# Rows set apart in the first loads and in one late store of an elementwise Huber loss, and a full second tile

## The chip, the cores and the metric

The kernel runs on one core of one Trainium2 chip. The metric is the device time of one execution in microseconds (us), lower is better. Below, a "row" is one partition's contiguous run of a tile in DRAM; the core's 16 DMA engines move rows between DRAM and the on-chip memory (SBUF).

## The reference

Two inputs of 8192 x 8192 float32 go in, one array of the same shape comes out, element by element:

```python
def reference(pred, target):
    delta = 1.0
    diff = pred - target
    abs_diff = np.abs(diff)
    return np.where(abs_diff <= delta, 0.5 * diff**2, delta * (abs_diff - 0.5 * delta))
```

So 536.87 MB are read and 268.44 MB are written, and there is no reuse of data.

## The kernel before

The kernel treats each array as one flat run of 67,108,864 floats and cuts it into 37 tiles of 128 rows. Tile `i` takes `128 * widths[i]` consecutive floats; its row `p` is `widths[i]` floats long and goes to partition `p`. The widths are 9408 (`GAP`), then 12000, then 34 times 14592 (`W`), then 6752.

All tiles share one SBUF buffer `mem` of 3 x 14592 + 9408 = 53184 floats per partition. The target of a tile is loaded into its "b" place (`at_b`: the first 14592 floats for even tiles, the next 14592 for odd tiles). The pred goes into its "a" place (`at_a`: even tiles from float 29184 on, odd tiles at the end of the buffer). The difference, and later the result, stand in the b place; the a place also serves as scratch once pred has been subtracted. The a places of neighbouring tiles overlap by up to `R` = 5184 floats; `covered(i)` gives the part of tile `i`'s a place that tile `i + 1` will overwrite. That part is subtracted first (`pieces`, `work`), so that the next tile's pred may be loaded while the rest of tile `i` is still being computed.

The arithmetic of a piece has five instructions on two engines: `subtract` (VectorE tensor_tensor, L95, then ScalarE Abs, L96), `square` (VectorE clamp to [-1, 1], L100, then ScalarE Square with scale sqrt(0.5), L103) and `combine` (VectorE scalar_tensor_tensor, max of |d| - 0.5 and that square, L107).

All loads (L80) and stores (L85) are issued by SyncE (SP), in program order: `load(0)`, `load(1)`, then for each tile `i`: `store(i - 1)`, `load(i + 1)` (inside `work(i)`, after the covered part has been subtracted), and at the end the store of the last tile. A load of pred is issued when the overlapped parts of the a place have been used; a load of target waits until the store that reads the same b place has landed, two tiles back. SP handles its queue in order, so whatever waits holds back everything issued later.

`parts(i)` says in which column ranges a tile is loaded: whole, except for the first tile and the last two (in halves) and the third from the end (two unequal parts). The last tile is also stored in halves. The order of work is written out by hand; waits between engines and DMAs are put in from the regions that overlap. The completion marks of the DMAs issued by SP are kept on eight semaphores in rotation: the ninth DMA uses the semaphore of the first again, and waits until that one has landed.

Of the kernel before, what the change touches and what calls it, by code (L numbers as in the profile page):

```python
# [1 line left out]

# [4 lines left out]


@with_exitstack
def kernel(  # L10
    ctx: ExitStack,
    tc: tile.TileContext,
    pred: bass.AP,
    target: bass.AP,
    out: bass.AP,
):
    nc = tc.nc
    P = 128
    fp32 = mybir.dt.float32
    Alu = mybir.AluOpType  # L20
    Act = mybir.ActivationFunctionType
    SQRT_HALF = 0.70710678118654752

    total = pred.shape[0] * pred.shape[1] // P
    W = 14592
    GAP = 9408
    R = W - GAP
    widths = [GAP, W - R // 2] + [W] * 34
    widths.append(total - sum(widths))
    n = len(widths)  # L30
    starts = [sum(widths[:i]) * P for i in range(n)]

    def block(x, i):
        flat = x.rearrange("r m -> (r m)")
        return flat[starts[i] : starts[i] + P * widths[i]].rearrange("(p m) -> p m", p=P)

    pool = ctx.enter_context(tc.tile_pool(name="memory", bufs=1))
    mem = pool.tile([P, 3 * W + GAP], fp32, name="mem")

    def at_a(i):
        return 3 * W + GAP - widths[i] if i % 2 else 2 * W

    def at_b(i):
        return W if i % 2 else 0

    def covered(i):  # L50

        if i + 1 >= n:
            return (0, 0)
        lo = max(at_a(i), at_a(i + 1))
        hi = min(at_a(i) + widths[i], at_a(i + 1) + widths[i + 1])
        return (lo - at_a(i), hi - at_a(i)) if hi > lo else (0, 0)


    def parts(i):
        w = widths[i]  # L60
        if i == n - 3:
            return [(w - 2 * R, w), (0, w - 2 * R)]
        if i in (0, n - 2, n - 1):
            return halves(w)
        return [(0, w)]

    def halves(w):
        h = w // 32 * 16
        return [(0, h), (h, w)]

    def view(base, lo, hi):
        return mem[:, base + lo : base + hi]

    def load(i):
        order = [(x, part) for part in parts(i) for x in "pt"]
        if i == n - 1:
            order = [(x, part) for x in "pt" for part in parts(i)]
        for x, (lo, hi) in order:
            src, base = (pred, at_a(i)) if x == "p" else (target, at_b(i))
            nc.sync.dma_start(out=view(base, lo, hi), in_=block(src, i)[:, lo:hi])  # L80

    def store(i):
        w = widths[i]
        for lo, hi in halves(w) if i == n - 1 else [(0, w)]:
            nc.sync.dma_start(out=block(out, i)[:, lo:hi], in_=view(at_b(i), lo, hi))  # L85

    def split(lo, hi, size):
        k = -((lo - hi) // size)
        edges = [lo + (hi - lo) * j // k // 16 * 16 for j in range(k)] + [hi]
        return list(zip(edges[:-1], edges[1:]))  # L90


    def subtract(i, lo, hi, at):
        a, d = view(at_a(i), lo, hi), view(at_b(i), lo, hi)
        nc.vector.tensor_tensor(out=d, in0=a, in1=d, op=Alu.subtract)  # L95
        nc.scalar.activation(out=d, in_=d, func=Act.Abs)  # L96

    def square(i, lo, hi, at):
        d, t = view(at_b(i), lo, hi), view(at_a(i) + at, 0, hi - lo)
        nc.vector.tensor_scalar(  # L100
            out=t, in0=d, scalar1=-1.0, scalar2=1.0, op0=Alu.max, op1=Alu.min
        )
        nc.scalar.activation(out=t, in_=t, func=Act.Square, scale=SQRT_HALF)  # L103

    def combine(i, lo, hi, at):
        d, t = view(at_b(i), lo, hi), view(at_a(i) + at, 0, hi - lo)
        nc.vector.scalar_tensor_tensor(  # L107
            out=d, in0=d, scalar=-0.5, in1=t, op0=Alu.add, op1=Alu.max
        )

    def pieces(i, lo, hi):


        c0, c1 = covered(i)
        c0, c1 = max(lo, c0), min(hi, c1)
        if c1 <= c0:
            k = -((lo - hi) // (R // 2 if i < n - 1 else R // 4))
            return [], [(i, x, y, x) for x, y in split(lo, hi, -((lo - hi) // k))]
        x, y = (lo, c0) if c0 > lo else (c1, hi)
        m = max(c1 - c0, (y - x) // 32 * 16)  # L120
        rest = [(x, x + m), (x + m, y)] if y > x + m else [(x, y)]
        return [(i, c0, c1, x)], [(i, x, y, x) for x, y in rest]

    def work(i, then):

        todo, held = [], []
        for part in parts(i):
            first, rest = pieces(i, *part)
            todo += first + rest
            held += first  # L130
        mid, end = [], []
        if held:
            subtract(*todo.pop(0))
        then()
        while todo or mid or end or held:
            if todo:
                piece = todo.pop(0)
                subtract(*piece)
                mid.append(piece)
                if len(mid) < 2 and todo:  # L140
                    continue
            if mid:
                piece = mid.pop(0)
                square(*piece)
                end.append(piece)
                if len(end) < 2 and (todo or mid):
                    continue
            combine(*end.pop(0))
            mid += held
            held = []  # L150

    ctx.enter_context(tc.manual_schedule())

    load(0)
    load(1)
    for i in range(n):
        if i > 0:
            store(i - 1)
        work(i, lambda: load(i + 1) if 0 < i < n - 1 else None)
    store(n - 1)  # L160


# [1 line left out]
_INS = ['pred', 'target']  # L164
_OUTS = [((8192, 8192), 'float32')]


# [23 lines left out]
```

## Time and profile before

| What | Value |
|---|---|
| median of 3 runs | 1867.21 us (1866.58 to 1867.41) |
| the profiled execution | 1866.7 us |
| its span, first to last instruction | 1864.9 us |
| VectorE (DVE) busy | 1408.3 us, 76% |
| ScalarE (ACT) busy | 912.5 us, 49% |
| GpSimd (POOL) busy | 0.2 us |
| DMA under way on the 16 engines | 99.9% of 16 engines' span |
| moved | 805.37 MB, mean 432 GB/s |

The profile comes from one execution, and the program's own instructions fill the span; 1.8 us of the execution's time lie around it. The share of DMA time is a mean over 16 engines: a stretch in which half of them have nothing left counts as half. The packet records behind these sums give start, length and size of each row's transfer, and one 4-byte packet for each engine's completion mark of each DMA.

### The profile page before, as it was taken

To read this page: it belongs to the slowest core of one execution; us is meant where nothing else is said; L and a number is where in the kernel's file an instruction comes from. 1 tells how busy PE (TensorE), PEld (TensorE's weight loads), DVE (VectorE), ACT (ScalarE), POOL (GpSimd) and SP (SyncE) were. 2 spreads that over 40 slices of the span, in tenths; PEclk is the share of its full clock that TensorE was granted. 3 is DMA by queue.
4 is the path that set the end of the run, shared out by engine and by line. 5 is a ranking of instruction groups with operands and counts; after the bars stand their busy time and mean duration, and the time that the engine had idled before them with its cause. 6 is when DMAs were issued, how large, how long until landed. Compare 5 with 4: busy or idle time off the path is not lost.

```text
span 1864.9 us, 960 instructions
## 1 busy us (share of the span) xinstructions
DVE 1408.3 (76%) x357; ACT 912.5 (49%) x239; POOL 0.2 (0%) x4
## 2 busy tenths in 40 slices
DVE  5677777777788777777778877777777887777986
ACT  3455444444555545444455554544445555454554
POOL 0000000000000000000000000000000000000000
DMA  9999999999999999999999999999999999999999
GB/s 421 418 436 431 436 431 432 437 427 436 438 428 434 439 428 435 438 429 433 438 428 436 438 428 435 438 428 436 438 427 437 436 429 437 435 429 436 428 437 393
DMA packets 17287, 805.37 MB, mean 432 GB/s; under 512 B 1920, under 2 KB 1920, under 8 KB 1920
## 3 DMA queue, kind: packets, MB, share of 16 engines
q1 hardware_dynamic: 17280, 805.31, 99.9%
q14 instruction: 7, 0.06, 0.0%
HBM read 536.87 MB, written 268.44 MB: 432 GB/s over the span
## 4 chain that ended last, share of the span: by engine, by line
DMA 56%; DVE 26%; ACT 13%; issue 4%; another core or an unknown queue 1%; SPq 0%; DVEq 0%
DMA mem<-in_target_dram 32%; DMA out_dram<-mem 24%; DVE mem L107 11%; DVE mem L95 11%; ACT mem L103 8%; ACT mem L96 4%; DVE mem L100 3%; SPq L80 0%; DVEq L95 0%
## 5 line engine op out<-in xcount | busy, mean ns | idle before, releaser
L96 ACT ACTIVATE mem<-mem 128x5184 f32<-128x5184 f32 (+8 forms) x119 | 459.2, 3874 | 756.3 <-DVE mem L95 756.2
L95 DVE TENSOR_TENSOR mem<-mem 128x5184 f32<-128x5184 f32 (+8 forms) x119 | 558.5, 4743 | 336.2 <-DMA mem<-in_target_dram 336.2
L107 DVE SCALAR_TENSOR_TENSOR mem<-mem 128x5184 f32<-128x5184 f32 (+8 forms) x119 | 564.4, 4745 | 74.5 <-ACT mem L103 70.6
L103 ACT ACTIVATE mem<-mem 128x5184 f32<-128x5184 f32 (+8 forms) x119 | 456.7, 3864 | 169.2 <-DVE mem L100 169.2
L100 DVE TENSOR_SCALAR mem<-mem 128x5184 f32<-128x5184 f32 (+8 forms) x119 | 292.0, 2453 | 34.9 <-ACT mem L96 29.9
L96 ACT ACT_TABLE_LOAD x1 | 1.3, 1283 | 14.6 <-DMA mem<-in_target_dram 14.6
L175 POOL MEMSET const-bfloat16-1.0<- 128x1 bf16 x1 | 0.1, 103 | 0.0
L175 POOL MEMSET const-uint8-127<- 128x1 uint8 x1 | 0.1, 102 | 0.0
L175 POOL MEMSET const-float32-0.0<- 128x1 f32 x1 | 0.1, 100 | 0.2 <-issue 0.2
L175 POOL MEMSET const-float32-1.0<- 128x1 f32 x1 | 0.1, 99 | 0.0
## 6 DMA issues: line engine op xcount, KB each, us to landing
out_dram<-mem SPq DMA_DIRECT2D x34, 7296.0 KB, 26.5
mem<-in_pred_dram SPq DMA_DIRECT2D x32, 7296.0 KB, 28.7
mem<-in_target_dram SPq DMA_DIRECT2D x32, 7296.0 KB, 34.4
mem<-in_pred_dram SPq DMA_DIRECT2D x2, 3648.0 KB, 27.6
mem<-in_target_dram SPq DMA_DIRECT2D x2, 3648.0 KB, 25.5
mem<-in_pred_dram SPq DMA_DIRECT2D x1, 6000.0 KB, 36.8
mem<-in_target_dram SPq DMA_DIRECT2D x1, 6000.0 KB, 51.5
out_dram<-mem SPq DMA_DIRECT2D x1, 6000.0 KB, 24.6
```

Source lines behind the costliest of these rows:

```text
L95: nc.vector.tensor_tensor(out=d, in0=a, in1=d, op=Alu.subtract)
L96: nc.scalar.activation(out=d, in_=d, func=Act.Abs)
L100: nc.vector.tensor_scalar(out=t, in0=d, scalar1=-1.0, scalar2=1.0, op0=Alu.max, op1=Alu.min)
L103: nc.scalar.activation(out=t, in_=t, func=Act.Square, scale=SQRT_HALF)
L107: nc.vector.scalar_tensor_tensor(out=d, in0=d, scalar=-0.5, in1=t, op0=Alu.add, op1=Alu.max)
L175: nc = _bacc.Bacc("TRN2", target_bir_lowering=False, num_devices=1)
```

## The change

Four places change.

The widths become 9408, 34 times 14592, 13056 and 5696. So the second tile is a full one, the last but one is 13056 instead of 14592 wide, and the last one is 5696 instead of 6752 wide. There are still 37 tiles.

The second tile is loaded in two column parts, 10368 and 4224 wide.

Of the first tile's four loads (pred and target of two halves), the first three are each issued as three DMAs: rows 0 to 111, rows 112 to 119, and rows 120 to 127.

The store of the last tile but one is split by rows. SP stores rows 0 to 111. GpSimd stores rows 112 to 119 and rows 120 to 127, each as two DMAs: the first 16 floats of each row, then the rest of the row.

```diff
-    widths = [GAP, W - R // 2] + [W] * 34
+    widths = [GAP] + [W] * 34 + [13056]
     widths.append(total - sum(widths))
...
     def parts(i):
         w = widths[i]
+        if i == 1:
+            return [(0, 2 * R), (2 * R, w)]
         if i == n - 3:
             return [(w - 2 * R, w), (0, w - 2 * R)]
...
-        for x, (lo, hi) in order:
+        for k, (x, (lo, hi)) in enumerate(order):
             src, base = (pred, at_a(i)) if x == "p" else (target, at_b(i))
-            nc.sync.dma_start(out=view(base, lo, hi), in_=block(src, i)[:, lo:hi])
+
+            apart = i == 0 and k < 3
+            for r0, r1 in [(0, 112), (112, 120), (120, 128)] if apart else [(0, P)]:
+                nc.sync.dma_start(
+                    out=mem[r0:r1, base + lo : base + hi], in_=block(src, i)[r0:r1, lo:hi]
+                )
 
     def store(i):
         w = widths[i]
+        if i == n - 2:
+
+            todo = [(nc.sync, 0, 112, 0, w)]
+            for r in (112, 120):
+                todo += [(nc.gpsimd, r, r + 8, 0, 16), (nc.gpsimd, r, r + 8, 16, w)]
+            for queue, r0, r1, lo, hi in todo:
+                queue.dma_start(
+                    out=block(out, i)[r0:r1, lo:hi],
+                    in_=mem[r0:r1, at_b(i) + lo : at_b(i) + hi],
+                )
+            return
         for lo, hi in halves(w) if i == n - 1 else [(0, w)]:
             nc.sync.dma_start(out=block(out, i)[:, lo:hi], in_=view(at_b(i), lo, hi))
```

## The prediction

> **What bounds the kernel now.** I read the page first: its sums, then the chain of waits.
>
> ```profile
> span 1864.9 us, 960 instructions
> ...
> DVE 1408.3 (76%) x357; ACT 912.5 (49%) x239; POOL 0.2 (0%) x4
> ...
> DMA packets 17287, 805.37 MB, mean 432 GB/s; under 512 B 1920, under 2 KB 1920, under 8 KB 1920
> ...
> q1 hardware_dynamic: 17280, 805.31, 99.9%
> ...
> DMA 56%; DVE 26%; ACT 13%; issue 4%; another core or an unknown queue 1%; SPq 0%; DVEq 0%
> ```
>
> The engines have slack, the DMA engines none: 99.9% of their time is taken. The chain runs through DVE and ACT for 39%, but only because one releaser at a time is followed back; behind each such piece the DMA queue is still full. So a change pays or costs only where DMA engines stand still, slow down, or end unevenly. Next, the table by stretches (busy DVE, ACT, POOL, clock, DMA share, GB/s), for where that happens:
>
> ```profile
> 0.00:1.60 1.60, 0.00 (x0) 0.00 (x0) 0.20 (x4) 1.00 0.00 0
> 1.60:15.00 13.40, 0.36 (x1) 0.39 (x1) 0.00 (x0) 1.00 1.01 414
> ...
> 51.00:55.00 4.00, 0.00 (x0) 0.00 (x0) 0.00 (x0) 1.00 1.07 343
> ...
> 410.00:1500.00 1090.00, 827.10 (x190) 530.57 (x126) 0.00 (x0) 1.00 1.00 434
> ...
> 1859.00:1861.00 2.00, 0.00 (x0) 0.00 (x0) 0.00 (x0) 1.00 0.85 358
> 1861.00:1863.60 2.60, 0.00 (x0) 0.00 (x0) 0.00 (x0) 1.00 0.36 151
> 1863.60:1864.90 1.30, 0.00 (x0) 0.00 (x0) 0.00 (x0) 1.00 0.00 0
> ```
>
> Nothing moves for 1.6 us, the rate is low in the first stretch and around 51 to 55 us (343 GB/s), steady at 434 later, and in the last 4.6 us the share falls to 0.85 and 0.36: engines have run out one by one. The packet records give the rest. A row's time is bytes / 27.2 per ns + about 9 ns: 0.70 us for 18,816 bytes, 1.39 for 37,632, 2.154 for 58,368, 0.505 for 13,504. Each DMA has 16 completion marks, 8 rows for each. The 16 marks of one DMA lie 0.84 us apart at 25 us, 0.92 at 54, 1.85 at 150, 2.84 at 254, 3.3 at 409, and the last ones 3.47 (1860.14 to 1863.62, mean 1861.82). So the engines, which have equal work, drift apart by slow packets, nearly all before 410 us and where loads turn into stores (51, 147, 200, 251 us), and the last engine ends 1.8 us after the mean. Slow packets sum to 2.9 us per engine, 1.1 of it in the one stall at 51 to 55 us.
>
> Last, how early each transfer is queued (timeline of SP's issues, then the chain near the end):
>
> ```profile
> 106.69 0.33 SPq L80 DMA_DIRECT2D mem<-in_pred_dram  x1
> 115.30 0.33 SPq L80 DMA_DIRECT2D mem<-in_target_dram  x1
> 143.40 0.34 SPq L85 DMA_DIRECT2D out_dram<-mem  x1
> ```
>
> ```profile
> 1789.19 33.52 DMA out_dram<-mem
> 1822.72 12.08 DMA mem<-in_target_dram
> ```
>
> The pred load issued at 106.69 has the store before it ending at 113.65 on the first engine: 7.0 us of cover. The store issued at 143.40 finds the load before it ending from 148.29 on: 4.9 us. The first load shows about 1.0 us from issue (0.73) to first packet (1.74), so 6.0 and 3.9 remain. These are what a wider spread of the engines uses up.
>
> **The change part by part.**
>
> *Bytes.* All widths still sum to 524,288, so 805.31 MB remain. Two more DMAs for the second tile (256 rows) and 16 short GpSimd rows are 272 more packets: 272 / 16 x 6 ns (9 ns less a 3 ns overlap) = +0.1 us per engine.
>
> *Rows set apart at the start.* A packet is a whole row, so a group of 8 rows occupies at most 8 of the 16 engines. Bounds: the groups fall on different engines in turn (no engine gains), or 8 rows on one engine (6 groups x 8 x 0.70 = 34 us). I take one row on each of the same eight engines, with 112 rows as 7 on all 16. Then per load eight engines carry 9 rows and eight carry 7: over three loads 3 x 0.70 = 2.1 us more for the "late eight" and 2.1 less for the "early eight", 4.2 us apart. [...]
>
> SP issues six more DMAs, 6 x 0.42 (its first issues' median) = 2.5 us. They lie beside 5.6 us of rows per load; without that cover they would cost 2.5. New waits come with them: semaphores rotate by eight, so the ninth DMA waits for the first. That lands at 2.3 + 7 x 0.70 = 7.2 us, while the early eight hold 21 rows, until 17. The sixth DMA, the last such wait among the loads, lands at 2.3 + 18 x 0.70 = 14.9; queued behind it is only the second target part of tile 1, which engines reach after 45 us. Tile 0's arithmetic starts 1.4 us later (2 rows; 14.64 before). Its store was issued at 44.92, 9 us ahead of need, and now has more loads in front: no cost.
>
> *The second tile full and in two parts.* The pred of tile 2 must wait for the covered part (2592 before, 5184 now). The first part lands at 2.3 + 2.1 + 32 x 0.70 + 16 x 1.53 = 51.3 us on the late eight; +0.4, +5.5 for one subtraction (11.04 / 2 in the chain) and it is issued at 57.2. The early eight have 16 x 0.63 + 8 x 1.39 = 21 us queued after their 47.1, so until 68: cover 11 us where it was 65.07 - 58.21 = 6.9. Hidden; uncovered, the sum would grow by what exceeds 11.
>
> *Steady tiles.* A spread of 4.2 + 0.84 = 5.0 us instead of 1.85 to 3.4: the 6.0 us of the pred load were measured at a spread of 1.25 and shrink by up to 3.8 to about 2.2, the store's 3.9 at 1.85 by up to 3.2 to 0.7. Nothing stands still, narrowly. The work of a tile (39.4 us of DVE in 51.7) does not change.
>
> *The gain.* Engines of the two sets no longer turn from loads to stores at once. Bounds: no slow packet is saved (0), or the drift goes, and all end within the first 0.84 us: 1860.14 + 0.84 + 0.1 = 1861.1 against 1863.62, -2.5 us (-3.6 with the 51 us stall too). I take most of the drift gone, -2.3, as it stopped once the marks lay 3.3 us apart.
>
> *The late store.* Rows are 13056 x 4 / 27.2 = 1.92 us. SP's part gives every engine 7 rows instead of 8; GpSimd's large groups give two more to some eight. If these are the early eight, they gain 1.92 and the late lose 1.92: the 4.2 us are undone but for 0.4. [...] GpSimd's four issues have no row; each between 0.33 (SP's) and 2 us (SP's slowest, 0.97, doubled) is at most 8 us, beside 13.5 us of SP's rows. If they are later than that, the end moves by the excess.
>
> *The tail's cover.* From the landing of tile 34 (1753.21 on the last engine) to the store of tile 35 (1831.85) lie 78.6 us, of which 42.7 are tile 35's arithmetic; in the same stretch transfers take 85.1 us (1749.75 to 1834.87, first engine). After: transfers 2 x 17.2 + 32 x 0.97 + 32 x 0.43 = 79.2, arithmetic 35.9 + 42.7 x 13056 / 14592 = 74.1. The first engine's cover goes from 85.1 - 78.6 - 3.5 = 3.0 to 79.2 - 74.1 - 5.0 = 0.1, less 1.0 for the issue: the early eight stand still for about 0.9 us, +0.7 net of what the late eight still have in hand.
>
> *Sum.* +0.1 (in the gain already) - 2.3 + 0.7 = -1.6 on 1866.7 (span 1864.9 to 1863.3): 1865.1 profiled. The median lies 0.5 above that profile: 1865.6.
>
> **The rivals.**
>
> *The stall at 51 us goes too.* For it: all 16 engines slow within one stretch, at the first turn from load to store, and are now apart there. Against: it may belong to the first store, whenever it comes. -1.1 more, and the tail's 0.7 not spent: 1863.8; with the 0.5 of run-to-run, 1863.3.
>
> *The late rows fall on the same eight.* Then the late eight end 2.1 + 1.9 later than an even share: 1861.1 + 4.0 = 1865.1 in the span, +1.5: 1868.7. Nothing in the profile speaks against it; GpSimd issues no DMA there.
>
> *Slower: neighbouring rows slow one another.* Before, each engine had its own rows in every DMA, and no row took less than its bytes / 27.2. If the eight rows of a group share paths into SBUF, each takes longer: bounds 0.70 (no sharing) and 8 x 0.70. With four to a path, 2.8 us: six groups cost the late eight 6 x 2.1 = 12.6 us more, two groups of stores cost the other eight 2 x 3 x 1.92 = 11.5 us. 1865.6 + 12 = 1878. The sets would be 16.8 us apart, past the 6 us of cover, so the early eight would also stand still for up to 10: 1888. It decides from about 1.1 us per row of a group on (6 x 0.4 eats the gain). [...]
>
> **How the numbers follow.** Forecast 1865.6 (own range 1863.5 to 1868): 0.42. Stall gone too, 1863.3: 0.14. Same eight, 1868.7: 0.15. Shared paths, 1878 to 1888: 0.29. 0.2% is 3.7 us, about what a measurement can tell from no change: 1863.5 to 1870.9 counts as the same. Faster: 0.11 of the second case and 0.03 of the first, 0.14. Slower: 0.29, and 0.03 of the third: 0.32. The same: 0.54. Range 1862.8 to 1884, which leaves out 0.03 below and some 0.13 above.
>
> **What would show it.** Completion marks of tile 0's loads about 5 us apart (17 if paths are shared); 18,816-byte rows of the groups at 0.70 us or at 2.8; spread constant through the middle; last marks within 1.5 us, the last two stretches of the table shorter; GpSimd's rows under way before 1850 us; a DMA share of 1.00 between. A share below 0.98 in the steady tiles, or group rows over 1.1 us, would make the prediction wrong.

## The result and the profile after

| Kernel | Median of 5 runs, us | Range |
|---|---|---|
| before | 1866.91 | 1866.46 to 1867.41 |
| changed | 1907.52 | 1905.33 to 1910.76 |

The changed kernel takes 1.022 times as long (95% interval 1.0208 to 1.0231): 40.6 us more, far above the forecast and above its range. The page of the changed kernel shows the same bytes, and VectorE and ScalarE as busy as before. Its second section gives the rate in 40 equal slices of 47.7 us:

```profile
span 1907.2 us, 995 instructions
...
DVE 1408.8 (74%) x363; ACT 913.0 (48%) x243; POOL 2.4 (0%) x8
...
DMA  9999999999999999999999999999999999999996
GB/s 236 436 435 431 431 432 438 436 432 433 433 431 435 439 434 432 432 432 431 435 441 433 432 431 432 432 435 438 436 432 431 431 431 431 437 425 436 414 421 219
...
q1 hardware_dynamic: 17600, 804.48, 98.9%
q0 software_dynamic: 128, 0.84, 0.3%
```

The first slice moves 236 GB/s (421 before), the last 219 (393 before); everything between is within a few per cent of what it was (414 the lowest, at the end). But the DMA row reads 9 in the first slice all the same, and q1 is busy for 98.9%. A row under way counts as busy even when it moves slowly (a share of 1.00 at 229 GB/s from 20 to 45 us), so here the loss shows in the GB/s and hardly in the busy share. The table by stretches of the changed kernel (length, busy DVE, ACT, POOL, clock, DMA share, GB/s):

```profile
2.00:10.00 8.00, 0.00 (x0) 0.00 (x0) 0.00 (x0) 1.00 1.08 275
10.00:20.00 10.00, 0.00 (x0) 0.00 (x0) 0.00 (x0) 1.00 0.92 181
20.00:45.00 25.00, 6.42 (x3) 7.66 (x4) 0.00 (x0) 1.00 1.00 229
...
50.00:1780.00 1730.00, 1314.21 (x311) 845.42 (x206) 0.00 (x0) 1.00 1.00 433
1780.00:1830.00 50.00, 45.88 (x20) 33.78 (x15) 0.00 (x0) 1.00 0.98 409
...
1862.00:1878.00 16.00, 5.52 (x6) 4.63 (x5) 0.00 (x0) 1.00 0.98 288
1878.00:1890.00 12.00, 10.90 (x12) 6.64 (x7) 0.00 (x0) 1.00 0.68 215
1890.00:1906.00 16.00, 0.00 (x0) 0.00 (x0) 0.00 (x0) 1.00 0.36 142
```

The same three first stretches of the kernel before:

```profile
2.00:10.00 8.00, 0.00 (x0) 0.00 (x0) 0.00 (x0) 1.00 0.93 388
10.00:20.00 10.00, 5.36 (x3) 3.65 (x3) 0.00 (x0) 1.00 1.01 433
20.00:45.00 25.00, 20.14 (x10) 14.61 (x7) 0.00 (x0) 1.00 1.04 448
```

From 2 to 45 us the changed kernel moves 8 us x 113 GB/s + 10 x 252 + 25 x 219 = 8.9 MB less, at 434 GB/s some 20 us. By the bytes in the packet records it is 19.9 us behind at 50 us, 18.8 at 60 (the stall of the kernel before at 51 to 55 us does not occur here), 19.2 at 1780 and 21.9 at 1858. The last row ends 42.2 us later than before, so another 20 us are lost at the end. The packet records name the rows: those of 18,816 bytes take 1.16 us in the median and up to 2.9 (0.70 before); SP's 112 rows of the late store take 1.93 to 4.4 us and GpSimd's sixteen 1.93 to 11.4, with a median of 6.3. What the 18,816-byte rows take beyond 0.70 us, added up from 4 us on and divided by the 16 engines, is 19.7 us (0.05 before): the loss at the start is in the rows themselves.

At the end a wait comes on top. The chain near the end of the changed kernel (start, length):

```profile
1814.55 36.92 DMA out_dram<-mem
...
1851.85 26.39 DMA mem<-in_target_dram
...
1878.34 1.14 DVE mem L113
```

The second half of the last tile's target needs 26.4 us from issue to landing. VectorE stands idle for it for 10.6 us, until 1878.34, and the last tile's stores come that much later, which is the share of 0.68 and 0.36 above. In the kernel before, the two halves were issued 0.4 us apart and landed after 12.1 (the one in the chain that the prediction shows) and 15.7 us, and nothing waited for the second. The list of issues from 1820 to 1865 us of the kernel before has the median of the two:

```profile
mem<-in_target_dram SPq DMA_DIRECT2D x2, 1688.0 KB, 13.9
```

### The profile page after: what moved, and what is told of

It reads as the page before. It is cut to its first block, busy times and chain, and to the rows that moved or that the text cites. A ratio compares the mean times of both kernels' runs of the same rounds, so it can differ in the third digit from the quotient of the medians.

```text
span 1907.2 us, 995 instructions
## 1 busy us (share of the span) xinstructions
DVE 1408.8 (74%) x363; ACT 913.0 (48%) x243; POOL 2.4 (0%) x8
## 3 DMA queue, kind: packets, MB, share of 16 engines
q1 hardware_dynamic: 17600, 804.48, 98.9%
## 4 chain that ended last, share of the span: by engine, by line
DMA 58%; DVE 25%; ACT 12%; issue 4%; SPq 0%; DVEq 0%
DMA mem<-in_target_dram 34%; DMA out_dram<-mem 24%; DVE mem L125 11%; DVE mem L113 11%; ACT mem L121 8%; ACT mem L114 4%; DVE mem L118 3%; SPq L85 0%; DVEq L113 0%
## 5 line engine op out<-in xcount | busy, mean ns | idle before, releaser
L114 ACT ACTIVATE mem<-mem 128x5184 f32<-128x5184 f32 (+8 forms) x121 | 459.6, 3813 | 776.1 <-DVE mem L113 776.0
L125 DVE SCALAR_TENSOR_TENSOR mem<-mem 128x5184 f32<-128x5184 f32 (+7 forms) x121 | 564.7, 4669 | 73.1 <-ACT mem L121 69.2
L121 ACT ACTIVATE mem<-mem 128x5184 f32<-128x5184 f32 (+7 forms) x121 | 457.1, 3803 | 169.0 <-DVE mem L118 169.0
L118 DVE TENSOR_SCALAR mem<-mem 128x5184 f32<-128x5184 f32 (+7 forms) x121 | 292.3, 2415 | 33.2 <-ACT mem L114 28.2
## 6 DMA issues: line engine op xcount, KB each, us to landing
out_dram<-mem SPq DMA_DIRECT2D x34, 7296.0 KB, 26.5
```

Of the source, the lines that this page charges most:

```text
L118: nc.vector.tensor_scalar(out=t, in0=d, scalar1=-1.0, scalar2=1.0, op0=Alu.max, op1=Alu.min)
L125: nc.vector.scalar_tensor_tensor(out=d, in0=d, scalar=-0.5, in1=t, op0=Alu.add, op1=Alu.max)
```

## The experiments

The theory (A), which the runs are to test: engines that work on a DMA with fewer than 128 rows get in one another's way at shared paths into SBUF. The rivals have letters too, and each expectation says what it means by them. Each experiment changes one thing in the kernel before; of each edit only the lines that say what differs are shown. Times are medians beside runs of the kernel before on the same chip, with the ratio's 95% interval.

**The parts of the change alone.** First, only the rows set apart at the start:

```diff
+            apart = i == 0 and k < 3
+            for r0, r1 in [(0, 112), (112, 120), (120, 128)] if apart else [(0, P)]:
```

> Only the first three loads are split by rows (112, 8, 8); the rest is as before. Theory A (shared paths: a DMA whose rows do not cover all partitions evenly makes several engines wait for the same path into SBUF): the start loses what the changed kernel lost by 50 us, 18 to 19 us of DMA time, and the whole comes out at 1884 to 1888 us. Rival B (the wider spread of the engines harms the steady tiles or the tail): under 10 us of it at the start, the rest later. Rival C (the new waits on the rotating semaphores): same 18 us, but with a DMA share below 0.95 in the first 40 us.

1893.23 against 1867.17 us, ratio 1.0135 (1.0114 to 1.0155). The profiled run, the longest of the four (1896.04), is 20.6 us behind at 50 us: somewhat more than A's 18 to 19, and against rival B. The DMA share is 1.08, 0.94 and 1.00 in the three stretches from 2 to 45 us, 1.00 in the mean, against rival C. The total is above A's 1884 to 1888: 19.5 us behind at 60 us, this run is 24.5 behind at 1780, so its middle loses 5 us. In the changed kernel, with the new widths and the split second tile, the same stretch loses 0.4. Which of the two saves the rest was not tried.

Then only the late store:

```diff
+            todo = [(nc.sync, 0, 112, 0, w)]
+            for r in (112, 120):
+                todo += [(nc.gpsimd, r, r + 8, 0, 16), (nc.gpsimd, r, r + 8, 16, w)]
```

> Only the store of the last tile but one is split by rows, with GpSimd's four DMAs; widths and loads as before (rows 14592 wide instead of 13056). Theory A: the end loses what the changed kernel lost after 1858 us, some 20 us, so 1883 to 1892. If start and end are independent, the sum of this loss and that of the start alone is the 40.6 us of the change to within 4 us. Rival D (GpSimd's queue was slow only because the engines arrived spread out): under 1872.

1889.62 us, ratio 1.0114 (1.0099 to 1.0129): the end is slow without any spread from the start, so rival D falls. The table by stretches of this kernel:

```profile
50.00:1780.00 1730.00, 1316.85 (x308) 850.76 (x206) 0.00 (x0) 1.00 1.00 433
1780.00:1834.00 54.00, 46.91 (x20) 30.42 (x13) 1.77 (x4) 1.00 1.00 430
1834.00:1850.00 16.00, 8.60 (x9) 6.20 (x6) 0.41 (x1) 1.00 1.07 319
1850.00:1870.00 20.00, 10.53 (x10) 6.84 (x7) 0.00 (x0) 1.00 0.84 250
1870.00:1886.00 16.00, 0.00 (x0) 0.00 (x0) 0.00 (x0) 1.00 0.28 104
```

From 1834 on the rate drops first with all engines busy (319 GB/s at a share of 1.07), then with engines out of work. The two losses add to 26.1 + 22.4 = 48.5 us, not to the 40.6 of the change: the expectation that they add within 4 us failed. The middle of the first kernel, which the changed kernel does not lose, may be some 5 us of the difference; the rest is open.

Then only the widths and the two parts of the second tile:

> Only the widths and the two parts of the second tile change. Theory A: no DMA with fewer than 128 rows, so 1865 to 1869, no difference that can be told. Rival E (the narrower tail leaves the engines without work near the end): 1869 to 1873, with a share of DMA below 0.97 between 1800 and 1850 us.

1867.19 us, ratio 1.0001 (0.9991 to 1.0010): nothing, so rival E falls.

**As many DMAs, cut by columns.** The first three loads go as three DMAs each, but of 128 rows:

```diff
+            cuts = [lo, hi - 592, hi - 288, hi] if i == 0 and k < 3 else [lo, hi]
+            for c0, c1 in zip(cuts[:-1], cuts[1:]):
+                nc.sync.dma_start(out=view(base, c0, c1), in_=block(src, i)[:, c0:c1])
```

> The first three loads are each split into three DMAs by columns instead of by rows: as many DMAs on SP and the same rotation of eight semaphores as with rows, but every DMA has 128 rows. Theory A: 1866 to 1869, rows at bytes / 27.2. Rival C (number of DMAs, waits on semaphores): 1880 or more, as with rows.

1867.41 us, ratio 1.0002 (0.9992 to 1.0011). Rival C falls: as many DMAs, with SP's issues and the rotation of the semaphores, cost nothing when each has 128 rows.

**Equal work for every engine, fewer rows.** Halves of 64 rows, four of each half for every engine if they are dealt out evenly:

```diff
+            for r0, r1 in [(0, 64), (64, 128)] if apart else [(0, P)]:
```

> The first three loads are each split into rows 0 to 63 and 64 to 127, the rest as before. Every engine has the same work (4 rows of each half), so no engine gets ahead by count. Theory A (shared paths, sixteen engines on half of the paths at a time): 18,816-byte rows at about 1.4 us instead of 0.70, 3 x 5.6 = 17 us lost, 1882 to 1888. Rival F (only the unequal numbers of rows for the engines harm): 1865 to 1870, rows at 0.70.

1884.73 against 1867.22 us, ratio 1.0095 (1.0080 to 1.0110). The table by stretches of this kernel:

```profile
10.00:20.00 10.00, 0.00 (x0) 0.00 (x0) 0.00 (x0) 1.00 1.00 211
20.00:30.00 10.00, 3.80 (x2) 2.44 (x2) 0.00 (x0) 1.00 1.01 211
```

The rate is half of 433 at a full DMA share: engines are busy and move at half speed. The rows' median is 1.45 us, 2.06 times 0.70, and the engines stay together (marks 1.1 us apart), so rival F, unequal work, falls. What the 18,816-byte rows take beyond 0.70 us comes to 16.5 us per engine, of the 17.5 that the kernel loses.

112 and 16 rows, seven and one for each engine if they are dealt out evenly:

```diff
+            for r0, r1 in [(0, 112), (112, 128)] if apart else [(0, P)]:
```

> The first three loads are each split into rows 0 to 111 and 112 to 127. 112 rows are 7 for each engine and 16 rows one for each, so all engines have equal work. Theory A: the sixteen last rows share few paths, about 2.8 us for 0.70, and the 112 rows cost what they did in the changed kernel, some 8 us for 4.9: 3 x 5 = 15 us, 1879 to 1886, completion marks under 2 us apart afterwards. Rival F (unequal numbers): 1865 to 1870.

1881.49 us, ratio 1.0077 (1.0060 to 1.0094). The first mark of the 112 rows comes 7.4 us after the first packet, where eight rows took 6.0 before; and in the second load the last engine's seven rows take 7.9 us (12.39 to 20.25) instead of 7 x 0.70 = 4.9. So 112 rows are slow by themselves. The same sum over the rows is 13.1 us, of 14.3 lost.

**Neighbours or not.** Six extra DMAs of eight rows load part of the first tile once more into free space, two behind each of the first three loads (0.9 MB, 2.1 us at 434 GB/s); either with eight neighbouring rows or with rows four apart:

```diff
+                for rows in (slice(64 + 16 * k, 72 + 16 * k), slice(72 + 16 * k, 80 + 16 * k)):
+                    nc.sync.dma_start(
+                        out=mem[rows, 9408 : 9408 + hi - lo], in_=block(src, i)[rows, lo:hi]
+                    )
```

> Before plus six extra 8-row DMAs at the start (two behind each of the first three loads), which load rows of the first tile once more into a part of the buffer that is not in use yet: 0.9 MB more. The rows are eight neighbours each (64 to 71, 72 to 79, up to 111). Same rows for each engine as in the next kernel. Theory A: four engines to a path, 2.8 us for a row, 6 x 2.8 = 17 us on the engines that carry them, the others wait for part of it: 1876 to 1888. Rival F (only the number of rows of an engine counts): 6 x 0.70 = 4.2 us, 1869 to 1872.

The other one has `slice(s, s + 29, 4)`, with s = 64 to 67, 96 and 97.

> The same six extra 8-row DMAs, but with rows four apart (64, 68, up to 92, and so on) instead of neighbours: same bytes, same number of rows per DMA, same engines by count. Theory A with paths that four neighbouring rows share: eight different paths, each shared with one other engine at most, 0.7 to 1.4 us for a row, 4 to 8 us: 1870 to 1876, and at least 6 us less than with neighbours. Rival G (a DMA of only eight rows is slow whatever its rows are): the same as with neighbours.

Neighbours: 1884.51 against 1867.07 us, ratio 1.0095 (1.0080 to 1.0110). Four apart: 1876.35 us, ratio 1.0048 (1.0031 to 1.0064), 0.35 us above the range that was expected. Same bytes, same count of rows and DMAs, 8.2 us between them; six rows at theory A's four and two times 0.70 us would make, by an estimate, 6 x (2.8 - 1.4) = 8.4. The slowest rows in the packet records fit: from 4 us on, 3.1 us with neighbours and 1.4 four apart. That the sums agree so closely is in part chance: what the rows take beyond 0.70 us adds up to 14.3 us per engine with neighbours and 4.2 four apart, 10.1 us between them. The stretch from 2 to 45 us, first with neighbours:

```profile
2.00:45.00 43.00, 7.57 (x4) 7.66 (x4) 0.00 (x0) 1.00 1.01 291
```

and with rows four apart:

```profile
2.00:45.00 43.00, 17.32 (x9) 13.80 (x7) 0.00 (x0) 1.00 1.00 385
```

The kernel before moves 433 there. Rival G (eight rows are slow whatever they are) and rival F fall.

That the shared place lies at SBUF is argued, not shown: rows that are neighbours in SBUF are neighbours in DRAM too, and no run parts the two. Against mere closeness in DRAM speaks that 128-row loads keep their speed at every distance between rows that the kernel before has, from 27,008 bytes (last tile, 0.505 us for 13,504 bytes) to 58,368 (2.154 us a row), while 64 and 112 rows are slow at the first tile's 37,632, where 128 rows take 0.70 us.

**GpSimd or the rows.** First SP issues all three row groups of the late store, without GpSimd:

```diff
+            todo = [(nc.sync, 0, 112, 0, w), (nc.sync, 112, 120, 0, w), (nc.sync, 120, 128, 0, w)]
```

> The store of the last tile but one is split into rows 0 to 111, 112 to 119 and 120 to 127, all by SP, no GpSimd. Theory A: the loss is that of the rows, as with GpSimd (22 us), 1884 to 1892. Rival D (GpSimd's own queue is slow): under 1873.

1885.42 against 1867.22 us, ratio 1.0096 (1.0081 to 1.0111), and single rows of up to 15.5 us instead of 2.15. So stores, which read SBUF, are slowed as loads are, and 18 us of the store's 22 come without GpSimd; rival D falls. Theory A's four times would make 4 x 2.15 = 8.6 us of a row; why seven rows here take 8.8 to 15.5 is open. Then GpSimd issues the whole store, 128 rows in one DMA:

```diff
+            todo = [(nc.gpsimd, 0, 128, 0, w)]
```

> The whole store of the last tile but one (128 rows) is issued by GpSimd in one DMA. Theory A: every engine reads its own rows, 1866 to 1871, rows of 58,368 bytes at 2.15 us. Rival D (GpSimd's own queue is slow): 1880 or more, rows well over 2.15 us.

1871.11 us, ratio 1.0021 (1.0012 to 1.0030): its rows keep their 2.15 us, as A has it, yet 3.9 us are lost. The chain near the end of this kernel says where:

```profile
1823.38 26.48 DMA mem<-in_target_dram
...
1849.96 1.33 DVE mem L104
```

The second half of the last target load, already waiting in SP's queue, lands 26.5 us after issue instead of the 15.7 of the kernel before; the first half lands as before (12.0). From 1835 us on the rows of GpSimd's queue, issued 9 us later (1832.39), take turns with it: rows of the load start at 1835.85, 1838.50, 1841.15 and 1843.80, 2.65 us apart, which is one row of 0.505 us and one of GpSimd's of 2.154. The records name no engine; by the spacing these rows are on one. The last tile is computed later, and the engines run dry before its stores.

**The stall at 51 to 55 us.** As it did not occur with a slowed start, one early write of 16 floats per row of the first tile's output was tried:

```diff
     load(1)
+    nc.gpsimd.dma_start(out=block(out, 0)[:, 0:16], in_=view(at_b(0), 0, 16))
```

> Before plus one early DMA from GpSimd that writes 16 floats of each row of the first tile's output (written again, rightly, by that tile's store). Theory H: the 1.1 us in which all engines stand at 51 to 55 us belongs to the first write into the output, whenever it comes; then it moves to 14 us or vanishes beside other work, and the time is 1 us lower, 1865.8 to 1866.5. Rival I: it belongs to something else (the turn from loads to the store of whole rows): 1866.9 to 1867.6 and the low rate at 51 to 55 us stays.

1867.08 against 1867.26 us, ratio 1.0000 (0.9991 to 1.0009). This kernel's stretch reads as before:

```profile
51.00:55.00 4.00, 0.00 (x0) 0.00 (x0) 0.00 (x0) 1.00 1.06 343
```

Theory H fell. With the wider second tile alone the low rate comes later, 393 GB/s at 55 to 61 us and 444 at 51 to 55, so it goes with the end of the first loads; yet the halves kernel, whose engines also turn from loads to the first store together, shows no such slow rows (its marks within 0.7 us from 42 to 216 us). What the stall comes from stays open, and no kernel here beats the one before.

## Why the prediction was wrong

**What bounds the kernel** was right: nothing in the middle moved, 433 GB/s from 50 to 1780 us.

**The step that failed** is "I take one row on each of the same eight engines" at 0.70 us a row, with the 112 rows "as 7 on all 16" at the same price, and likewise 1.92 us a row in the late store. What was to move time between engines for nothing cost 19.9 us by 50 us, and the end another 20. That a group of eight rows lies on eight engines, and 112 rows on all 16, the packet records bear out: eight completion marks for each of SP's groups, sixteen for the 112 rows. The halves, the neighbours and the rows four apart show that here a row's time depends on which rows move at the same time: 0.70 us in a DMA of 128 rows, 1.3 to 1.45 where theory A has two engines to a path, up to 3.1 where it has four. The forecast took the bound without sharing because every row in the trace had 0.70; but every DMA in it had 128 rows, so that trace could not tell. The rival "neighbouring rows slow one another" had the right direction, with a chance of 0.29: six extra groups cost 17.4 us with neighbours (1884.51 us) and 9.3 four apart (1876.35). Its four to a path, from which its 2.8 us a row follow, no run shows; what the runs show in its place are rows of up to 3.1 us with neighbours, up to 1.4 four apart, and 211 GB/s, half of 433, with halves of 64 rows.

**The size of that rival** (1878 to 1888) was too small for three reasons. It let only the groups of eight share paths and left the 112 rows at their old speed; with 112 and 16 rows, and no group of eight, 14 us are lost, of which the 112 rows have about 3 x 3 by an estimate. At the end it let SP's 112 rows keep 1.93 us, and they took up to 4.4. And it had GpSimd's rows lie beside SP's store, when, as the 128 rows from GpSimd show, they also take turns with the load queued ahead of it. The spread of 16.8 us that it feared did not come: the marks are 5.3 us apart after the start. The engines without group rows were slowed too: some 11 us lie between the marks of the first load's 112 rows (9.2 to 9.9 us) and the eight earliest marks of the second's (20.1 to 21.2), where seven rows at 0.70 us make 4.9. That 5.3 is near the forecast's 5.0 is chance, since its 4.2 were worked out from rows at 0.70 us.

**The gain** of 2.3 us never had a chance to show. The spread was indeed wider through the middle (5.3 us at 60 us, 7 at 1700), and engines still drifted. So keeping the sets apart did not stop the drift. Nor did turning together start it: in the halves kernel every engine turned from loads to stores together, and the marks stayed within 0.7 us from 42 to 216 us; they drifted later, to 6.4 by 1714. The cause of the drift was not tried by itself.

**The steps with no cost** held. SP's extra issues and the rotating semaphores: nothing, by columns. Widths and the split second tile: 0.0 us, alone. The steady tiles' cover was enough, as worked out. GpSimd's issues took 0.64 us and 1.54 for three, not up to 8.

**The tail's cover** had the right sign: engines stood still between 1780 and 1830 us (share 0.98), and 2.3 us were lost from 1780 to 1830, where 0.7 were forecast, with marks up to 8.3 us apart instead of the 5.0 assumed. The spread counts for more than the narrower tail: with the old tail the slow start alone loses 1.2 us in the same stretch, and the new tail alone costs nothing.

**The late store** was to undo the 4.2 us. GpSimd's rows took three times as long (6.3 us in the median, against 1.92), and the last marks are 11 us apart where 1.5 were expected. That GpSimd's groups fall on the early eight was the author's assumption: on which engines they fell, the trace does not show.

## What to carry to other kernels

Where every DMA in a trace has the same shape, its row times hold for that shape only: before rows are divided otherwise, measure one DMA of the new shape. Cut a transfer by columns, which is free here (1867.41 against 1867.17 us), and leave all 128 rows in each DMA; here a DMA that evens out the engines by row counts paid two to four times per row (1.45 us in halves, up to 3.1 with neighbours, for 0.70), and more in the store (up to 15.5 for 2.15). Read the GB/s beside the DMA share: a share of 1.00 also stands over half the rate (211 GB/s with halves of 64 rows).

## What the runs showed of the hardware

- Stores, which read SBUF, were slowed by row groups as loads were: with the store's rows grouped by SP alone, single rows of 58,368 bytes took up to 15.5 us instead of 2.15.
- A later DMA on GpSimd's queue delayed one that already waited on SP's queue: 26.5 us to landing instead of 15.7 with the 128-row store from GpSimd. Rows of the load start 2.65 us apart there, one of its own (0.505 us) and one of GpSimd's (2.154).
- 112 rows were slower in all than 128: first mark 7.4 us after the first packet against 6.0.
- All engines stood for about 1.1 us at 51 to 55 us in the kernel before (343 GB/s), not in those with a slow start; a first small write into the output, made early, did not remove it (343 GB/s again).
